# Modulation sums through turned 32x32 blocks on VectorE, and gate rows through DRAM, in a hybrid diffusion layer

## The chip, the cores and the metric

The kernel runs on one core of a Trainium2 chip. The metric is device time in microseconds (us) of one execution. A core has five engines that each follow their own instruction stream in order: TensorE (PE; its weight loads are listed apart, as PEld), VectorE (DVE), ScalarE (ACT), GpSimd (POOL) and SyncE (SP). DMA transfers are issued from queues on SP, ACT and POOL. An engine waits for another through semaphores.

## The reference

One layer for two groups of tokens, 256 context tokens (`x_prompt`) and 2048 latent tokens (`x_sample`), with model width 1024, all in float32. What matters here is the modulation. Each group has one conditioning vector, and a small matmul makes six vectors of 1024 numbers from it, which are used in every row of the group:

```python
def adaln(cvec, w_mod, b_mod):
    m = jax.nn.silu(cvec) @ w_mod + b_mod          # (1024,) @ (1024, 6144)
    return jnp.split(m[:, None, :], 6, axis=-1)

sh1, sc1, g1, sh2, sc2, g2 = adaln(c, w_mod[l], b_mod[l])
h = rms_norm(xs, norm1_g[l]) * (1 + sc1) + sh1
q, k, v, f = project(h, w_in[l], q_norm_g[l], k_norm_g[l])
...
mix = merge(attn, fourier_mix(f, w_four[l]), subln_g[l], lam_init, w_out[l])
xs = xs + g1 * mix
h = rms_norm(xs, norm2_g[l]) * (1 + sc2) + sh2
xs = xs + g2 * sq_relu_mlp(h, w1[l], w2[l])
```

The same is done for the context tokens with `c_ctx`. `sh1` and `sc1` are needed before the first projection, `g1` after the output projection, `sh2` and `sc2` for the second norm, and `g2` at the very end.

## The kernel before, in words

The 2304 tokens are 18 tiles of 128. The stages follow each other:

1. A short setup (to about 62 us) loads the first quarter of `w_mod`, makes modulation groups 0 to 3 (a group is 512 of the 6144 columns) and splits the projection weights.
2. The projection stage (about 62 to 468 us) runs a loop `for i in range(1, LAST)` over the tiles. A tile has four projections `proj(i, g)` of 24 matmuls each into four PSUM banks named `pj` (tag with four buffers), for q, k, v and the Fourier channels. Each float32 product is three matmuls of split operands (`mm3`, L87 to L89). The banks are read by `squares` (L250, L251, L254, the power on POOL at L255), `qk_norm` (`qn`, L268), `v_out` (L356) and `f_post`; when the next tile starts its projection 0, it needs the bank that `qn` of the tile before has read. Beside that the loop loads the next x tile, norms it (L187 to L191), transposes it (`pta`, L200), and stores q, k and v to DRAM.
3. The Fourier stage, attention (to about 1283 us), the output projection with the second norm (about 1283 to 1510 us), and a two-part MLP (the rest).

The loop of stage 2 is not in a written order: a scheduler lays out the instructions of each engine from a simulated timeline, so an edit can move neighbours. The output projection and the last part of the MLP stand under `tc.manual_schedule()`, where the order is that of the text.

Modulation groups 4 to 11 are made in stage 2, one in every odd tile i, by `mod_group_v`. VectorE multiplies each of eight row blocks of the weights (128x512) with a column of the conditioning vector and adds them up into `macc` (L164, L166), once for each of the two vectors s. What is left is the sum of `macc` over the 128 partitions. TensorE makes it: for each of four blocks of 128 columns a matmul with `macc` as weights and a column of ones as moving operand (L168) gives a column of 128 sums in `pm`. `mod_bias` (L142) adds the bias and puts the columns into `modc`, a 128x48x2 table: column c of it holds elements 128c to 128c+127 of the modulation vector.

The gates `g1` and `g2` multiply rows of tokens, so they are needed as a row of 1024 numbers repeated on all 128 partitions. `mk_gate` (L174 to L181) makes half a row: four matmuls, each with a column of `modc` broadcast to 128x128 as weights and the identity as moving operand, into a PSUM bank `pg`, and an ACT copy (L181) into the tile `g1[s]` or `g2[s]`. It is called four times in the output stage, between the matmuls `out_mm` (L1554, L1562, L1565, L1574) and four times early in the last stage (L1958). `out_post` (L1501) reads `g1`, `y_post` (L1902) reads `g2`.

Of the kernel before, what the change touches and what calls it, by code (L numbers as in the profile page):

```python
# [41 lines left out]
def body(tc, a, out):  # L42
    nc = tc.nc
    ctx = ExitStack()
    with ctx:
# [6 lines left out]
        def scratch(name, shape):  # L52
            return dram.tile(shape, F32, tag=name, name=name)
# [9 lines left out]
        four = scratch("four", [512, NT])  # L63
        xnew = [scratch(f"xnew{i}", [P, D]) for i in range(NT // P)]
        HB = NT // 2
        hop = [[scratch(f"hd{p}_{b}", [P, 4, 384]) for b in range(3)] for p in range(8)]
        tsum = [scratch(f"tsum{k}", [P, 3, 512]) for k in range(16)]
        sop = [[scratch(f"sd{p}_{b}", [P, 16, 384]) for b in range(3)] for p in range(8)]
# [71 lines left out]
        def mod_bias(gi, pm):  # L140
            b = cols[:, 32 + gi * 4:32 + gi * 4 + 4].unsqueeze(2).to_broadcast([P, 4, 2])
            nc.vector.tensor_add(modc[:, gi * 4:gi * 4 + 4, :], pm, b)  # L142
# [10 lines left out]
                nc.tensor.transpose(pm[:, j, :], r[0:2, j * P:(j + 1) * P], ident[0:2, 0:2])  # L153
            mod_bias(gi, pm)

        def mod_group_v(t2, pps, gi, w):

            pm = pps.tile([P, 4, 2], F32, tag="pm", name=f"pm{gi}")
            for s in range(2):
                acc = t2(f"macc{gi}_{s}")  # L160
                for k in range(KD):
                    wk, sc = w[k // 2][:, k % 2, :], cols[:, 8 * s + k:8 * s + k + 1]
                    if k == 0:
                        nc.vector.tensor_scalar_mul(acc, wk, sc)  # L164
                    else:
                        nc.vector.scalar_tensor_tensor(acc, wk, sc, acc, op0=ALU.mult, op1=ALU.add)  # L166
                for j in range(4):
                    nc.tensor.matmul(pm[:, j, s:s + 1], acc[:, j * P:(j + 1) * P], ones, start=True, stop=True)  # L168
            mod_bias(gi, pm)

        def mk_scale(dst, c0, gcol):
            nc.vector.tensor_scalar_add(dst, modc[:, c0:c0 + KD, :], 1.0)
            nc.vector.tensor_mul(dst, dst, cols[:, gcol:gcol + KD].unsqueeze(2).to_broadcast([P, KD, 2]))

        def mk_gate(pps, dst, c0, s, halves=(0, 1)):
            for hf in halves:
                pg = pps.tile([P, 512], F32, tag="pg", name=f"pg{c0}_{s}_{hf}", bufs=1)
                for j in range(4):
                    col = modc[:, c0 + hf * 4 + j, s:s + 1]
                    nc.tensor.matmul(pg[:, j * P:(j + 1) * P], col.to_broadcast([P, P]), ident, start=True, stop=True)  # L180
                nc.scalar.copy(dst[:, hf * 512:hf * 512 + 512], pg)  # L181

        def norm(pool, xt, nm, dst=None):

# [24 lines left out]
        with ExitStack() as c1:  # L209
# [28 lines left out]
            def proj(i, g):  # L238
                ps = pp.tile([P, 512], F32, tag="pj", name=f"pj{i}_{g}", bufs=4)
                hh, hl = HH[i]  # L240
                for k in range(KD):
                    mm3(ps, hh[:, k, :], hl[:, k, :], wh[g][k], wl[g][k], k == 0, k == KD - 1)
                PJ[i, g] = ps
# [172 lines left out]
            with tc.manual_schedule():  # L416
# [108 lines left out]
                v_split(1, 0, vo0, "v0")  # L525
                load(3)
            wm, LAST = None, N1 - 1
            for i in range(1, LAST):
                mg = 3 + (i + 1) // 2
                if i >= 2 + N1 // 2 - 1:  # L530
                    f_load(i)
                    if i > 2 + N1 // 2 - 1:
                        f_rev(i - 1)
                if i % 2 and mg < 12:
                    wm = mod_load(po, mg)
                if i > 1:
                    norm(p1, X[i + 1], f"a{i + 1}")
                    proj(i, 0)
                transposed(i + 1)
                if 1 < i < N1 - 2:  # L540
                    load(i + 2)
                squares(i, 0)
                if i > 1:
                    proj(i, 1)
                qk_T(i - 1)
                squares(i, 1)
                proj(i, 2)
                qk_post(i)
                v_post(i)
                proj(i, 3)  # L550
                f_post(i)
                if i % 2 and mg < 12:
                    mod_group_v(t2, pps, mg, wm)
                if i in (4, 6, 8, 10):
                    cache_tile((i - 4) // 2)
            mk_scale(scale2, 32, 88)
# [873 lines left out]
        with c3o, ExitStack() as c4, ExitStack() as c4x, ExitStack() as c4w:  # L1430
# [105 lines left out]
            with tc.manual_schedule():  # L1536
# [2 lines left out]
                mix_load(s1)  # L1539
                x_load(s0)  # L1540
                x_load(s1)
                w_split(1, 0, 1)
                mix(s0)
                w_split(1, 1, 4)
# [6 lines left out]
                    fn()  # L1551
                mix(s1)
                out_mm(s0, 1, 4)
                mk_gate(pp, g1[1], 16, 1, (1,))  # L1554
                w_split(0)
                kv_even.close()
                ms1 = ctx.enter_context(tc.tile_pool(name="m_s1", bufs=2, side="right"))
# [1 line left out]
                mix_load(s2)  # L1559
                x_load(s2)  # L1560
                out_mm(s1, 1)
                mk_gate(pp, g1[0], 16, 0, (1,))  # L1562
                out_post(s0, 1)
                out_mm(s0, 0)
                mk_gate(pp, g1[1], 16, 1, (0,))  # L1565
                out_post(s1, 1)
                mix(s2)
                out_post(s0, 0)
# [2 lines left out]
                mix_load(seq[3])  # L1571
                x_load(seq[3])
                out_mm(s1, 0)
                mk_gate(pp, g1[0], 16, 0, (0,))  # L1574
                out_post(s1, 0)
                x_store(s1)
                x_norm(s1)
# [284 lines left out]
        with ExitStack() as c6:  # L1862
# [62 lines left out]
            with tc.manual_schedule():  # L1925
                pend, NM, loaded, KS = None, 7 * 24, 4, []
                for i in range(7):
                    for b in range(3):
                        ps = [pp.tile([P, 512], F32, tag="ps", name=f"ps{i}_{b}_{j}", bufs=6) for j in range(3)]
                        for k in range(16):  # L1930
# [19 lines left out]
                            if (i, b) == (6, 2) and 9 <= k < 12:  # L1950
# [2 lines left out]
                                u = U3[6 + j]  # L1953
                                nc.vector.tensor_mul(u, u, g2[0][:, 0:512])
                                nc.vector.tensor_add(u, u, X[j])
                            if i == 0 and b == 1 and k in (2, 6, 10, 14):
                                s, hf = divmod(k // 4, 2)
                                mk_gate(pp, g2[s], 40, s, (hf,))  # L1958
                            KS.append((k, SO[m], TO[n]))
                            if i == 6 and b == 2 and 12 <= k < 15:  # L1960
                                continue
# [85 lines left out]
```

## Time and profile before

| | |
|---|---|
| median of 3 runs | 2914.43 us (2913.92 to 2915.5) |
| profiled execution | 2917.55 us, of which the span from first to last instruction is 2915.8 us |
| TensorE busy | 2877.5 us, 99% of the span |
| VectorE, ScalarE, GpSimd busy | 2022.7, 1564.2 and 1059.4 us |
| mean granted TensorE clock | 0.996 |
| chain that ended last | TensorE 91% |

How to read the rows that follow. A row of a timeline gives the start in us, the duration, engine, line of the kernel, operation, output<-input, shape and count; a bracket names how long the engine was idle before it and what ended that wait. A row of a group gives line, engine, operation, names, shapes, count, then busy us in total and mean ns of one, then idle time before it and its releasers. A row of a tile gives the least, median and largest duration in ns and the first and last start. Matmuls are pipelined, so the distance between two starts says more than a duration. A program matmul of float32 operands is two instructions in the trace.

### The profile page before, as it was taken

Reading aid. Unit: us, or ns where it says so; the run is one execution under the profiler, and the core shown is the slowest. Engines: PE = TensorE matmul, PEld = TensorE weight load, DVE = VectorE, ACT = ScalarE, POOL = GpSimd, SP = SyncE. Lnnn points to the kernel's source line nnn. Section 1 sums busy time; section 2 is a strip of 40 time slices with the busy share of each in tenths; the row PEclk is TensorE's granted clock in tenths of the full one; section 3 lists DMA queues with packets and bytes.
Section 4 is the critical chain, followed back from the end, with each engine's and each line's share of the span. In section 5 each row is a group of like instructions: output and inputs, shape, how many; then the busy total and the mean of one; then the engine's idle time right before and its main releaser. Section 6 shows DMA issues by size and latency. Waiting matters only on the chain.

```text
span 2915.8 us, 43832 instructions
## 1 busy us (share of the span) xinstructions
PE 2877.5 (99%) x15425; PEld 2501.2 (86%) x15425; DVE 2022.7 (69%) x3401; ACT 1564.2 (54%) x3524; POOL 1059.4 (36%) x865
## 2 busy tenths in 40 slices
PE   8999999999999999999999999999999999999999
PEld 4888888688888888888889999999998888888887
DVE  6666777989998988964468778778775344345554
ACT  4333323688998989964356566556554332232221
POOL 1111113398998999952213333333332000000000
PEclk9999999999999999999999999999999999999999
DMA  7777878621121201217777677676656364445663
GB/s 280 193 205 191 224 198 246 212 81 56 44 106 51 105 28 50 86 60 212 217 241 221 219 241 233 219 238 222 223 186 236 123 201 149 137 141 174 204 207 109
DMA packets 394415, 493.50 MB, mean 169 GB/s; under 512 B 26403, under 2 KB 307056, under 8 KB 391122
## 3 DMA queue, kind: packets, MB, share of 16 engines
q1 hardware_dynamic: 386560, 477.63, 52.0%
q10 hardware_dynamic: 4642, 7.88, 0.8%
q0 software_dynamic: 2992, 5.18, 0.6%
q8 instruction: 122, 2.00, 0.3%
q14 instruction: 99, 0.81, 0.1%
HBM read 313.11 MB, written 179.57 MB: 169 GB/s over the span
## 4 chain that ended last, share of the span: by engine, by line
PE 91%; DVE 3%; ACT 2%; DMA 1%; issue 1%; POOL 1%; SPq 0%; ACTq 0%; DVEq 0%; POOLq 0%
PE Ss L989 10%; PE ps L87 8%; PE ps L88 8%; PE ps L89 8%; PE pts L1044 4%; PE pj L87 4%; PE pj L88 4%; PE pj L89 4%; PE po L87 4%; PE po L89 4%; PE po L88 4%; PE pA L1654 2%; PE pA L1655 2%; PE pB L1655 2%; PE pB L1654 2%; PE pB L1656 2%
## 5 line engine op out<-in xcount | busy, mean ns | idle before, releaser
L994 DVE TENSOR_REDUCE mxs<-Ss 128x1 f32<-128x512 f32 x636 | 413.3, 685 | 65.2 <-PE Ss L989 53.0
L1329 DVE TENSOR_TENSOR sl<-sr,sh 128x768 fp32r<-128x768 f32 x168 | 161.8, 964 | 339.8 <-ACT sh L1328 339.3
L1029 POOL TENSOR_TENSOR P0s<-P0s,P1s 128x1024 f32<-128x1024 f32 (+2 forms) x128 | 377.0, 2945 | 10.7
L1328 ACT CAST sh<-sr 128x768 fp32r<-128x768 f32 x168 | 140.3, 836 | 424.7 <-PE ps L88 424.7
L1696 POOL TENSOR_TENSOR gs<-g,g 128x384 f32<-128x384 f32 x48 | 69.6, 1451 | 469.5 <-ACT g L1666 400.9
L1013 ACT ACTIVATE P1s<-Ss,mxs 128x512 f32<-128x512 f32 x318 | 215.4, 695 | 35.9 <-DVE mxs L997 34.5
L87 PE MATMUL pj<-wh,hh 128*128 128x512 f32 x576 | 229.6, 399 | 0.7 <-ACT fo L381 0.7
L88 PE MATMUL ps<-tlT,sh 128*128 128x512 f32 x585 | 229.3, 392 | 0.0
L87 PE MATMUL ps<-thT,sh 128*128 128x512 f32 x585 | 229.2, 392 | 0.0
L88 PE MATMUL pj<-wl,hh 128*128 128x512 f32 x576 | 227.7, 395 | 0.5 <-DVE wl L503 0.5
L89 PE MATMUL ps<-thT,sl 128*128 128x512 f32 x585 | 227.7, 389 | 0.0
L89 PE MATMUL pj<-wh,hl 128*128 128x512 f32 x576 | 226.6, 394 | 0.0
L1013 ACT ACTIVATE P0s<-Ss,mxs 128x512 f32<-128x512 f32 x318 | 214.4, 691 | 4.3 <-DVE mxs L997 3.6
L989 PE MATMUL Ss<-KS1s,Qs 128*128 128x512 f32 x636 | 196.4, 421 | 5.5 <-ACT P0s L1013 3.0
L989 PE MATMUL Ss<-KS0s,Qs 128*128 128x512 f32 x636 | 196.7, 422 | 2.6 <-ACT P1s L1013 2.4
L1044 PEld LDWEIGHTS pts<-ident,P0s 128*128 128x128 f32 x1280 | 158.2, 140 | 43.1 <-ACT ahs L1051 3.1
L1044 PE MATMUL pts<-ident,P0s 128*128 128x128 f32 x1280 | 191.0, 273 | 0.7 <-ACT P1s L1013 0.7
L1665 ACT ACTIVATE g<-uz 128x384 f32<-128x384 f32 x144 | 76.0, 528 | 200.1 <-DVE uz L1688 174.7
L1028 POOL TENSOR_SCALAR P1s<-P1s,tots 128x1024 f32<-128x1024 f32 (+2 forms) x128 | 172.0, 1344 | 5.8
L1056 DVE TENSOR_TENSOR als<-pts,ahs 128x512 fp32r<-128x512 f32 x256 | 165.9, 681 | 6.8 <-ACT ahs L1051 6.6
L87 PE MATMUL ps<-ophT,sh 128*128 128x512 f32 x423 | 165.9, 392 | 1.1 <-DVE uz L1688 1.1
L89 PE MATMUL ps<-ophT,sl 128*128 128x512 f32 x423 | 165.7, 392 | 0.0
(642 smaller groups left out, 8210.2 us busy)
## 6 DMA issues: line engine op xcount, KB each, us to landing
sr<-sd SPq DMA_DIRECT2D x84, 768.0 KB, 4.5
a<-in_w SPq DMA_DIRECT2D x184, 256.0 KB, 4.3
sd<-gs SPq DMA_DIRECT2D x192, 192.0 KB, 2.1
sd<-g SPq DMA_DIRECT2D x144, 192.0 KB, 4.5
wm<-in_w_mod SPq DMA_DIRECT2D x32, 512.0 KB, 5.7
Qs<-qd SPq DMA_DIRECT2D x32, 512.0 KB, 3.6
b<-in_w SPq DMA_DIRECT2D x64, 256.0 KB, 5.2
b<-tsum SPq DMA_DIRECT2D x64, 256.0 KB, 4.7
```

The lines of the kernel that those rows point to most:

```text
L87: nc.tensor.matmul(ps, lh, rh, start=first, stop=False)
L88: nc.tensor.matmul(ps, lh, rl, start=False, stop=False)
L89: nc.tensor.matmul(ps, ll, rh, start=False, stop=last)
L989: nc.tensor.matmul(S[:, :w], self.Q[:, x, m, j * P:j * P + P], self.hd.KS[m][:, b * 512:b * 512 + w], start=(x == 0), stop=(x == 1))
L994: nc.vector.tensor_reduce(self.mx[j][:, m, b:b + 1], self.S[j, m, b], axis=AX.X, op=ALU.max)
L1013: nc.scalar.activation(dst, S, AF.Exp, bias=self.mx[j][:, m, 6:7], accum_out=self.sm[j][:, m, b:b + 1])
L1028: nc.gpsimd.tensor_scalar(p, p, tot[:, 3:4], 0.0, op0=ALU.mult, op1=ALU.add)
L1029: nc.gpsimd.tensor_add(d, d, p)
L1044: nc.tensor.transpose(pt[:, c:c + P], self.p0[j][:, (kb + t) * P:(kb + t + 1) * P], ident)
L1056: nc.vector.tensor_sub(t, self.pt[kb], f32(self.A[kb][0]))
L1328: nc.scalar.copy(hi, src)
L1329: nc.vector.tensor_sub(lo, src, f32(hi))
```

## The change

`mod_group_v` keeps its accumulation on VectorE, and no longer uses TensorE. A `tensor_reduce` with `apply_transpose` takes `macc` as sixteen blocks of 32 columns; in each 32x32 block (32 partitions by 32 columns) it turns the block and sums, so that partition 32q+i of the output holds, for each block of columns c, the sum over the 32 partitions of quarter q of column 32c+i. The result is 128x16 for each s and goes into a tile `sums` that holds four groups.

What is left to add, over the four quarters, is done once for four groups, in tiles 8 and 16. `mod_sums` builds on GpSimd a 128x224 tile `quad`, zero but for four stacked 32x32 identities in columns 96 to 127 (a memset and three adds), and issues four matmuls, in which shifted windows of `quad` are the weights and every fourth column of `sums` (32 columns) is the moving operand. `mod_finish` adds the bias for all four groups in one VectorE instruction. `gate_store` transposes the sixteen gate columns of `modc` on TensorE, copies them on ScalarE, and stores them on ScalarE's queue, with one DMA for each s, to a scratch tensor `gates` in DRAM.

`mk_gate` and its eight calls go. Instead `gate_load` reads one row of 1024 numbers from DRAM with 128 partitions as destination, on SP's queue: two at the beginning of the output stage (behind the loads of the first x tiles, ahead of `mix_load(s2)`), and two in the last stage, at steps 2 and 10 of its second block.

```diff
+        gates = [scratch(f"gate{n}", [2, D]) for n in range(2)]
...
-        def mod_group_v(t2, pps, gi, w):
-            pm = pps.tile([P, 4, 2], F32, tag="pm", name=f"pm{gi}")
+        def mod_group_v(t2, sums, gi, w):
             for s in range(2):
                 acc = t2(f"macc{gi}_{s}")
...
-                for j in range(4):
-                    nc.tensor.matmul(pm[:, j, s:s + 1], acc[:, j * P:(j + 1) * P], ones, start=True, stop=True)
-            mod_bias(gi, pm)
+                nc.vector.tensor_reduce(sums[:, gi % 4, s, :], acc.rearrange("p (c i) -> p c i", i=32), axis=AX.X, op=ALU.add,
+                                        apply_transpose=True)
+
+        FIN = {}
+
+        def mod_sums(t2, pps, sums, gi):
+            z = t2(f"quad{gi}")[:, 0:224]
+            nc.gpsimd.memset(z, 0.0)
+            nc.gpsimd.tensor_add(z[:, 96:128], ident[:, 0:32], ident[:, 32:64])
+            for q in (2, 3):
+                nc.gpsimd.tensor_add(z[:, 96:128], z[:, 96:128], ident[:, 32 * q:32 * q + 32])
+            FIN[gi] = pm = pps.tile([P, 4, 2, 4], F32, tag="pm", name=f"pm{gi}")
+            for q in range(4):
+                nc.tensor.matmul(pm, z[:, 96 - 32 * q:224 - 32 * q], sums[:, :, :, q::4], start=(q == 0), stop=(q == 3))
+
+        def mod_finish(gi):
+            nc.vector.tensor_add(modc[:, gi * 4:gi * 4 + 16, :].rearrange("p (g j) s -> p g j s", j=4),
+                                 FIN.pop(gi).rearrange("p g s j -> p g j s"),
+                                 cols[:, 32 + gi * 4:48 + gi * 4].rearrange("p (g j) -> p g j", j=4).unsqueeze(3).to_broadcast([P, 4, 4, 2]))
+
+        def gate_store(t2, pps, n):
+            c0 = (16, 40)[n]
+            pr = pps.tile([P, 512], F32, tag="pg", name=f"pgate{n}")
+            gr = t2(f"gr{n}")
+            nc.tensor.transpose(pr[0:16, 0:P], modc[:, c0:c0 + 8, :].rearrange("p k s -> p (k s)"), ident)
+            nc.scalar.copy(gr[0:16, 0:P], pr[0:16, 0:P])
+            for s in range(2):
+                nc.scalar.dma_start(gates[n][s].rearrange("(k p) -> k p", p=P), gr[s:16:2, 0:P])
+
+        def gate_load(dst, n, s):
+            nc.sync.dma_start(dst, gates[n][s:s + 1, :].partition_broadcast(P).rearrange("p o d -> p (o d)"))
...
-        def mk_gate(pps, dst, c0, s, halves=(0, 1)):
...
@@ loop over the tiles of the projection stage
                 squares(i, 0)
                 if i > 1:
                     proj(i, 1)
+                fin = {8: 4, 16: 8}.get(i)
+                if fin:
+                    mod_sums(t2, pps, sums, fin)
                 qk_T(i - 1)
                 squares(i, 1)
                 proj(i, 2)
+                if fin:
+                    mod_finish(fin)
                 qk_post(i)
                 v_post(i)
                 proj(i, 3)
+                if fin:
+                    gate_store(t2, pps, fin // 8)
                 f_post(i)
                 if i % 2 and mg < 12:
-                    mod_group_v(t2, pps, mg, wm)
+                    mod_group_v(t2, sums, mg, wm)
@@ output stage
                 x_load(s0)
                 x_load(s1)
+                for s in (1, 0):
+                    gate_load(g1[s], 0, s)
...
                 out_mm(s0, 1, 4)
-                mk_gate(pp, g1[1], 16, 1, (1,))
...
                 out_mm(s1, 1)
-                mk_gate(pp, g1[0], 16, 0, (1,))
                 out_post(s0, 1)
                 out_mm(s0, 0)
-                mk_gate(pp, g1[1], 16, 1, (0,))
...
                 out_mm(s1, 0)
-                mk_gate(pp, g1[0], 16, 0, (0,))
@@ last stage
-                            if i == 0 and b == 1 and k in (2, 6, 10, 14):
-                                s, hf = divmod(k // 4, 2)
-                                mk_gate(pp, g2[s], 40, s, (hf,))
+                            if i == 0 and b == 1 and k in (2, 10):
+                                gate_load(g2[k // 8], 1, k // 8)
```

The scheduler lays stage 2 out anew. In its order for the changed program the two reduces of a group stand on VectorE ahead of L254 (the finish of the squares' sum) in tiles 2, 4, 6 and 16, and behind it in tiles 8 to 14; the four matmuls of `mod_sums` stand at the end of tile 8's last projection and inside tile 16's. The group loaded in tile i is finished in tile i+1.

7 lines of the change are left out of this document (1 added, 6 removed).

## The prediction

> **What bounds the kernel now.** I read the page first, then the busy time by stage, then the chain inside the stages that the change touches.
>
> ```profile
> PE 2877.5 (99%) x15425; PEld 2501.2 (86%) x15425; DVE 2022.7 (69%) x3401; ACT 1564.2 (54%) x3524; POOL 1059.4 (36%) x865
> PE 91%; DVE 3%; ACT 2%; DMA 1%; issue 1%; POOL 1%; SPq 0%; ACTq 0%; DVEq 0%; POOLq 0%
> 62.00:468.00 406.00, 405.31 (x1978) 337.39 (x1978) 281.19 (x523) 128.84 (x278) 64.87 (x32) 1.00 0.77 200
> 1280.00:1330.00 50.00, 49.17 (x256) 40.85 (x255) 30.20 (x46) 23.79 (x52) 10.98 (x12) 1.00 0.47 148
> 2270.00:2300.00 30.00, 30.00 (x141) 24.92 (x140) 10.89 (x14) 12.31 (x19) 0.00 (x0) 1.00 0.45 149
> ```
>
> In a window row the columns are the stretch, its length, the busy time of PE, weight load, DVE, ACT and POOL, then granted clock, DMA share and GB/s. TensorE carries 91% of the chain that ended last. In the projection stage (62 to 468 us) it is busy 405.3 of 406.0 us at full clock, while VectorE has 125 us free and ScalarE 277. The pieces of the change lie in this stage, at 1290 to 1311, and at 2261 to 2281. In all three a TensorE instruction taken out should bring the end nearer, unless something else is late next.
>
> ```profile
> by line: PE pj L87 29.8%; PE pj L89 29.7%; PE pj L88 29.6%; PE pta L200 3.5%; PE pm L168 3.3%; PE ptkT L310 1.7%; PE ptqT L310 1.7%; PE ptckT L310 0.4%; DVE fo L387 0.2%; ACT fo L381 0.1%; issue 0.0%
> 467.48 0.69 DVE L387 TENSOR_TENSOR fo<-fh,pj 128x512 f32<-128x512 f32 x1 [3.97 <-PE pj L89]
> ```
>
> The first line is the chain inside 62 to 468: TensorE throughout, the small modulation matmuls (L168) 3.3% of it. The second is the handover to the Fourier stage: VectorE had been idle 3.97 us waiting for the last projection. What the stage saves is therefore handed on.
>
> **Part 1: the modulation matmuls go.** Eight groups (4 to 11) each issue eight 128x1 matmuls, in the trace sixteen instructions.
>
> ```profile
> L168 PE MATMUL pm<-ones,macc x128: 165/250/250, 107.2 to 456.1; 128*128 128x1 f32 x128
> 106.94 0.39 PE L88 MATMUL pj<-wl,hh 128*128 128x512 f32 x1
> 107.17 1.84 PE L168 MATMUL pm<-ones,macc 128*128 128x1 f32 x16
> 108.87 0.48 PE L89 MATMUL pj<-wh,hl 128*128 128x512 f32 x1
> 109.19 0.39 PE L87 MATMUL pj<-wh,hh 128*128 128x512 f32 x1
> 94.79 0.87 PE pta L200 x8
> ```
>
> Starts are 0.23 apart in the stream (106.94 to 107.17). A group shifts the stream by 108.87 - 107.17 = 1.70, and the matmul after it takes 0.32 instead of 0.23, so 1.79 us. Eight groups: **-14.3 us**, all on the chain.
>
> In their place, after groups 7 and 11, come four matmuls with 32 columns (at two instructions each, eight) and one transpose. Their nearest rows: 1.70/16 = 0.106 us an instruction at one column, 0.87/8 = 0.109 at 128 columns (last line above, from the chain). Eight are 0.87, the transpose 0.11, two switches 0.09 each: 1.2 us, twice: **+2.4 us**.
>
> **Part 2: VectorE's reduces, and a wait that becomes tight.** VectorE gets sixteen reduces of 128x512 to 128x16 through turned 32x32 blocks, and loses six of eight small adds.
>
> ```profile
> L251 DVE TENSOR_REDUCE qss<-sq 128x8 f32<-128x512 f32 x34 | 23.0, 682 | 37.3 <-ACT sq L250 37.3
> L142 DVE TENSOR_TENSOR modc<-pm,cols 128x8 f32<-128x8 f32 x8 | 1.3, 158 | 1.0 <-PE pm L168 1.0
> L164 DVE TENSOR_SCALAR macc<-wm,cols 128x512 f32<-128x512 f32 x16 | 7.1, 482 | 0.0
> L166 DVE SCALAR_TENSOR_TENSOR macc<-wm,cols,macc 128x512 f32<-128x512 f32 x112 | 78.4, 747 | 15.8 <-DMA wm<-in_w_mod 15.8
> L255 POOL TENSOR_TENSOR qrs<-qss,mhalf 128x16 f32<-128x16 f32 x17 | 49.4, 2908 | 157.5 <-DVE qss L254 157.5
> ```
>
> The trace has no turned reduce. The plain one over the same 512 elements takes 0.68 us; I take that, with 0.48 as lower bound (L164's pass over 512) and 1.4 (two passes) as upper. 16 x 0.68 = 10.9 us against 125 us free: no throughput limit. But VectorE works in order, and after each tile's second projection its squares, their sum, the power on POOL (L255, 2.9 us) and `qn` (L268) must be through before TensorE may reuse the first of four `pj` banks for the next tile.
>
> ```profile
> 111.08 0.69 DVE L268 TENSOR_TENSOR qn<-pj,qrs 128x512 f32<-128x512 f32 x1 [1.87 <-POOL qrs L255]
> 114.69 0.39 PE L87 MATMUL pj<-wh,hh 128*128 128x512 f32 x1
> 211.35 0.69 DVE L268 TENSOR_TENSOR qn<-pj,qrs 128x512 f32<-128x512 f32 x1 [3.08 <-POOL qrs L255]
> 213.80 0.39 PE L87 MATMUL pj<-wh,hh 128*128 128x512 f32 x1
> 362.62 0.69 DVE L268 TENSOR_TENSOR qn<-pj,qrs 128x512 f32<-128x512 f32 x1 [3.09 <-POOL qrs L255]
> 363.92 0.47 PE L87 MATMUL pj<-wh,hh 128*128 128x512 f32 x1
> ```
>
> In each pair the bank comes free at the end of `qn` and TensorE starts on it in the next line. Slack: tile 2 114.69 - 111.77 = 2.9 us, tile 6 1.8, tile 12 0.6. The same pairs in tiles 4, 8, 10, 14 and 16 give 4.8, 2.1, 1.7, 3.8 and 4.7. Taking the L168 block out brings TensorE 1.79 us earlier to each of these points, and nothing in that chain gets faster. The order of the changed program puts the two reduces ahead of the sum's finish (L254) in tiles 2, 4, 6 and 16, which delays `qn` by 2 x 0.68 = 1.4; in tiles 8 to 14 they stand behind it and fit into the 3.1 us in which VectorE waits for POOL (the bracket above). New stalls: tile 2 1.79 + 1.37 - 2.9 = 0.2; tile 6 1.79 + 1.37 - 1.8 = 1.4; tile 10 0.1; tile 12 1.79 - 0.6 = 1.2; tile 8 none, since the new matmuls stand ahead of its bank. Sum **+2.9 us**. Bounds: 0 if the chain's start (an x load that TensorE's own transposes release) moves up too, 6 with the reduce at 1.4 us.
>
> **The rest of stage one.** POOL gets a memset and three 128x32 adds, twice.
>
> ```profile
> L815 POOL MEMSET jm<- 128x128 f32 x1 | 0.2, 233 | 0.0
> L694 POOL TENSOR_TENSOR ys<-yu 128x256 f32<-128x256 f32 x4 | 3.4, 843 | 0.0
> 317.84 0.33 ACTq L262 DMA_DIRECT2D rp<-in_rope  x1
> ```
>
> At most 0.4 + 3 x 0.84 = 2.9 us on an engine that is 16% busy and 341 us idle here; the next norm or `qrs` stands behind it, and the matmuls that need it come a whole projection later. Nothing, up to 1 us if `qrs` is caught behind it. ACT gets one copy and two DMA issues of about 0.4 (last line), twice; in the built program the second issue also waits for an earlier weight load. ACT's next work is the copies of `pj`, and it idled 277 us. Nothing. The new matmuls wait for the reduce of group 7 or 11 a projection (5.5 us) after it: nothing.
>
> **Part 3: the gate rows.** Eight halves of four matmuls (sixty-four instructions) and eight ACT copies go.
>
> ```profile
> 1290.36 1.05 PE L180 MATMUL pg<-ident,modc 128*128 128x128 f32 x8
> 1291.17 0.48 PE L87 MATMUL po<-woh,mh 128*128 128x512 f32 x1
> 1291.49 0.39 PE L88 MATMUL po<-wol,mh 128*128 128x512 f32 x1
> 1304.12 0.60 PE L1478 MATMUL po<-ident,am 128*128 128x128 f32 x4
> 1304.80 0.69 ACT L1479 ACTIVATE mT<-po,cols 128x512 f32<-128x512 f32 x1
> 1310.13 1.05 PE L180 MATMUL pg<-ident,modc 128*128 128x128 f32 x8
> 1311.82 1.09 PE L200 MATMUL ptb<-ident,xn 128*128 128x128 f32 x8 [0.63 <-DVE xn L191]
> L180 PE MATMUL pg<-ident,modc x64: 270/275/275, 1290.4 to 2280.7; 128*128 128x128 f32 x64
> 2271.00 0.89 PE pg L180 x8
> ```
>
> A half costs 1291.17 - 1290.36 = 0.81 plus 0.09 in the next matmul: 0.90 us. At the end the stream of four is unbroken: 4 x 0.90 = **-3.6 us**. In the output stage the first three stand ahead of the transposes at 1304.12, but the fourth stands in a stretch that ends with a wait: from 1304.72 (end of the transposes) runs mT, its split, out_post, norm, xn, and TensorE waited 0.63 us for it. Without the fourth half it only waits longer. 3 x 0.90 = **-2.7 us** (bounds -2.7 and -3.6).
>
> The rows come instead by four 512 KB loads on SP's queue.
>
> ```profile
> xo<-in_x_sample SPq DMA_DIRECT2D x1, 512.0 KB, 6.7
> 1281.64 0.43 SPq L1466 DMA_DIRECT2D am<-att  x1
> 1297.41 0.68 DVE L1501 TENSOR_TENSOR gt<-po,g 128x512 f32<-128x512 f32 x1
> L1902 DVE TENSOR_TENSOR c<-c,g x6: 691/692/694, 2353.9 to 2395.8; 128x512 f32<-128x512 f32 x6
> ```
>
> The first two take the place at 1281.64, ahead of am, mT and xo of the third tile, which move back by two issues of 0.43; am is first read at 1304. A load of that size lands in 6.7 us, the second near 1290; the first use is at 1297.41. Hidden, with 7 us over. The two at 2271 go between weight loads; the rows are first used at 2353.9. Nothing.
>
> **Sum.** -14.3 + 2.4 + 2.9 - 2.7 - 3.6 = -15.3 us. The profiled execution took 2917.55 us (its span 2915.8), 3.1 above the median of 2914.43; taken off the median: **2899.1 us**. By the bounds of the unknown terms: 2895.3 (no stalls, the fourth half counted) to 2902.2 (stalls of 6).
>
> **Rivals.** *Stage one keeps its length.* The chain of x load, squares, POOL and `qn` sets the pace of every pair of tiles, or the Fourier stage's own loads set when it starts, and all 11.9 us (14.3 - 2.4) are lost: 2914.4 - 6.3 = 2908.1. For it: the slacks of 0.6 to 2 us. Against: tiles 4, 14 and all without a group have 4 to 6 us, and VectorE waited 3.97 at the handover.
>
> *Slower: the turned reduce is dear.* A group's price X enters the chain twice; over the first seven pairs the stalls are about 7 x 1.79 + 14 X, less 3.09 hidden in four of them and 18.7 of slack: 14 X - 18.5 us. That eats the 18.2 us of the other terms at X = 2.6, and at X = 3.0 (4.4 times the plain row) the time is 2920. Per element nothing on VectorE in this trace is near that: 512 elements cost 0.48 to 0.75 us in every row. [...] No run here shows a turned reduce.
>
> *The gate loads are late.* They read one 4 KB row 128 times, which no load of this size in the trace does. TensorE stands still once they land after about 1303 (three `po` banks); at 30 us from issue instead of 6.7 it would lose 8 us: 2907.
>
> **Chances.** The sum 0.68 (its own range 2895 to 2902.5), stage one keeps its length 0.12, dear reduce 0.07, late loads 0.05, something unnamed 0.08. Within 0.2% (5.8 us), about what a measurement here can tell from no change, is 2908.6 to 2920.2: half of the second case and parts of the third and last, 0.09. Faster 0.82, slower 0.09. The range for 8 in 10 takes the sum's own bounds and the late loads: 2893.5 to 2907.
>
> **What would show it.** No L168 or L180 rows; TensorE's instructions down by about 170; turned reduces at 0.5 to 1.4 us; the projection stage 8 to 12 us shorter, with TensorE idle a few times before the first `pj` of a tile and `qn` as releaser (tiles 6 and 12 first); g loads landing before 1290 on the old clock; 3.6 us less in the last stage. The prediction is wrong if VectorE's reduces exceed 2 us, if the stall before `pj` appears in most tiles, or if the Fourier stage does not start as much earlier as the projections end.

## The result, and the profile after

The changed kernel takes 2908.06 us (median of 12 executions, 2905.58 to 2912.91). The kernel before took 2915.99 in the executions beside them (12, 2913.61 to 2918.93). The ratio is 0.9972, with a 95% interval of 0.9964 to 0.998: about 8 us less, where 15.3 were forecast, and 1.1 us above the range. The profiled execution took 2906.92 us, 1.1 below its median, with a span of 2905.1.

First the busy time on the page of the changed kernel, then two rows of its busy time by stage (the columns are those of the prediction), then the second stretch in the kernel before.

```profile
PE 2857.5 (98%) x15251; PEld 2482.1 (85%) x15251; DVE 2030.7 (70%) x3411; ACT 1557.9 (54%) x3518; POOL 1064.1 (37%) x873
```

```profile
62.00:468.00 406.00, 402.32 (x1907) 332.36 (x1906) 293.00 (x538) 130.69 (x282) 70.39 (x41) 1.00 0.77 202
468.00:560.00 92.00, 78.09 (x481) 66.20 (x479) 73.53 (x140) 40.35 (x95) 33.49 (x50) 0.93 0.81 262
```

```profile
468.00:560.00 92.00, 83.70 (x511) 72.39 (x509) 74.66 (x142) 39.67 (x90) 35.33 (x50) 0.94 0.82 260
```

TensorE has 174 instructions fewer and 20.0 us less to do, but the span is only 10.7 us shorter (and by the medians the time only 7.9, since the profiled execution before, 2917.55, lies 1.6 above its median). The second and third row show where to look: in the 92 us that hold most of the Fourier stage TensorE worked 5.6 us less than before, although nothing was taken out there.

The stage boundaries say it more exactly. These are rows of tiles (least, median and largest ns, then the first and the last start): the turned reduce; the first transposes after the projections (`ptqkT`), the first and last score matmul of attention (`Ss`), the first transposes of the second norm (`ptb`), the first matmul of the last stage (`tlT`), and the first of its last outputs (`cl`). First the kernel before, then the changed one.

```profile
L310 PE MATMUL ptqkT<-ident,qo x8: 270/272/273, 467.3 to 468.0; 128*128 128x128 f32 x8
L989 PE MATMUL Ss<-KS0s,Qs x636: 387/398/776, 555.7 to 1249.8; 128*128 128x512 f32 x159
L200 PEld LDWEIGHTS ptb<-ident,xn x136: 138/141/146, 1311.8 to 1504.7; 128*128 128x128 f32 x136
L88 PE MATMUL ps<-tlT,sh x585: 387/394/397, 2234.1 to 2909.4; 128*128 128x512 f32 x195
L1971 DVE TENSOR_TENSOR cl<-ps,g x3: 691/692/692, 2905.8 to 2911.4; 128x512 f32<-128x512 f32 x3
```

```profile
L167 DVE TRANSPOSE_TENSOR_REDUCE sums<-macc x16: 667/703/709, 107.0 to 446.2; 128x16 f32<-128x512 f32 x16
L331 PE MATMUL ptqkT<-ident,qo x8: 272/273/273, 459.0 to 459.8; 128*128 128x128 f32 x8
L1018 PE MATMUL Ss<-KS0s,Qs x636: 386/397/506, 553.2 to 1245.3; 128*128 128x512 f32 x159
L221 PEld LDWEIGHTS ptb<-ident,xn x136: 138/141/147, 1304.7 to 1497.7; 128*128 128x128 f32 x136
L89 PE MATMUL ps<-tlT,sh x585: 388/394/398, 2227.1 to 2898.7; 128*128 128x512 f32 x195
L1997 DVE TENSOR_TENSOR cl<-ps,g x3: 691/691/692, 2895.2 to 2900.8; 128x512 f32<-128x512 f32 x3
```

| up to | before | after | gained so far | in this stretch | forecast |
|---|---|---|---|---|---|
| first `ptqkT` | 467.3 | 459.0 | 8.3 | 8.3 | 9.0 |
| first `Ss` | 555.7 | 553.2 | 2.5 | -5.8 | 0 |
| last `Ss` | 1249.8 | 1245.3 | 4.5 | 2.0 | 0 |
| first `ptb` | 1311.8 | 1304.7 | 7.1 | 2.6 | 2.7 |
| first `tlT` | 2234.1 | 2227.1 | 7.0 | -0.1 | 0 |
| first `cl` | 2905.8 | 2895.2 | 10.6 | 3.6 | 3.6 |

Four of the six stretches come within 0.7 us of the forecast. The 2.0 us in attention were not forecast, and they do not follow the change: over the first 50 us of attention the granted clock was 0.97 in the kernel before and 1.00 in the changed one, and the longest `Ss` in the rows above took 776 and 506 ns. Of the kernels below, before_high and sums_high have a longest `Ss` of 776 ns, before_prep and gates_high of 506 and 505. From first to last `Ss` these last four take 694.1, 693.7, 692.3 and 692.0 us. The Fourier stage gives back 5.8 of the 8.3 us that the projections handed it. The place is found in the timeline of that stage; first the kernel before (GpSimd's first addition `ys`, L691, and two subtractions of VectorE that matter later), then the changed kernel (the issue of one store on SP's queue, the same addition, now L720, and the matmul that waited behind it).

```profile
507.93 0.74 POOL L691 TENSOR_TENSOR ys<-yd 128x256 f32<-128x256 f32 x1 [0.24 <-DVE yd L688]
508.48 0.73 DVE L579 TENSOR_TENSOR fpt0l<-etmp,fpt0h 128x512 fp32r<-128x512 f32 x1
508.63 1.19 POOL L692 TENSOR_TENSOR ys<-yd 128x256 f32<-128x256 f32 x1
509.14 1.23 DVE L579 TENSOR_TENSOR fpt1l<-etmp,fpt1h 128x512 fp32r<-128x512 f32 x1
```

```profile
493.74 0.37 SPq L370 DMA_DIRECT2D vd<-v17l  x1
498.83 0.53 POOL L612 DMA_DIRECT2D s<-in_s  x1 [0.32 <-DMA c<-in_c]
506.67 0.72 POOL L720 TENSOR_TENSOR ys<-yd 128x256 f32<-128x256 f32 x1 [7.31 <-DMA vd<-v17l]
510.11 0.79 PE L88 MATMUL pz<-abho,cwh 128*128 128x512 f32 x1 [4.17 <-ACT yu L706]
```

In the kernel before, GpSimd added as soon as `yd` was there. In the changed one it stood idle for 7.31 us until a transfer had landed that has nothing to do with the sum: the store of `v17l`, the low half of the last v tile, issued on SP's queue at 493.74. The copy `yu`, VectorE's next difference and TensorE's `pz` all waited behind it, TensorE for 4.17 us. The next rows of the changed kernel's busy time show what followed.

```profile
504.00:508.00 4.00, 1.94 (x14) 1.45 (x12) 0.00 (x0) 0.00 (x0) 1.33 (x2) 1.00 1.07 245
508.00:512.00 4.00, 1.65 (x3) 0.83 (x3) 1.81 (x3) 1.84 (x5) 4.00 (x7) 0.63 0.98 191
512.00:516.00 4.00, 3.12 (x5) 1.46 (x5) 4.00 (x6) 0.38 (x1) 4.00 (x5) 0.51 0.76 204
```

The column behind the busy times is the granted clock: 0.63 and 0.51 in the eight microseconds from 508 on, in the first two of which TensorE still stood.

Why a store and a sum that share no data meet is a matter of memory. In the built programs `ys0` occupies bytes 103392 to 111583 of every partition in both kernels; it is laid out when the projection stage's tiles are given up. From 109792 up lie the six buffers of the tag `t2r`, through which the halves of v, k and q are stored to DRAM. The first of the six, which `ys0` overlaps, held `qkT16_1h` last in the kernel before, and `v17l`, the last tile of this tag to be stored, in the changed one; in the kernel before `v17l` lay under `ys1`. Which buffer a tile gets follows from the order in which the scheduler's simulated timeline frees them, and with the change that order came out differently. The prediction looked at no addresses.

### The profile page after: what moved, and what is told of

Its sections match the earlier page's. It is cut to its first block, busy times and chain, and to the rows that moved or that the text cites. A ratio compares the mean times of both kernels' runs of the same rounds, so it can differ in the third digit from the quotient of the medians.

```text
span 2905.1 us, 43522 instructions
## 1 busy us (share of the span) xinstructions
PE 2857.5 (98%) x15251; PEld 2482.1 (85%) x15251; DVE 2030.7 (70%) x3411; ACT 1557.9 (54%) x3518; POOL 1064.1 (37%) x873
## 4 chain that ended last, share of the span: by engine, by line
PE 65%; issue 7%; POOL 4%; ACT 2%; DVE 2%; DMA 2%; SPq 0%; POOLq 0%; ACTq 0%; DVEq 0%
PE Ss L1018 10%; PE ps L89 8%; PE ps L88 8%; PE ps L90 8%; PE pts L1073 5%; PE po L90 4%; PE po L88 4%; PE po L89 4%; PE po L1099 2%; PE pB L1683 1%; PE pB L1682 1%; PE pB L1681 1%; PE pA L1682 1%; PE pA L1681 1%; POOL gs L1723 1%
## 5 line engine op out<-in xcount | busy, mean ns | idle before, releaser
L1058 POOL TENSOR_TENSOR P0s<-P0s,P1s 128x1024 f32<-128x1024 f32 (+2 forms) x128 | 378.7, 2959 | 10.7
```

The source lines that it names most:

```text
L1058: nc.gpsimd.tensor_add(d, d, p)
```

## The experiments

Theory A: this store holds the Fourier stage up. Theory B, a part of the prediction's first rival: the Fourier stage's own loads set when it starts, wherever its tiles lie. In all runs the kernel before ran beside them, with medians of 2915.7 to 2916.5 us.

**after_high: the overlap taken away.** The four `ys` tiles are laid out in the opposite order, so that `ys0` lies at the top and the two tiles written last meet `v17h` and `v17l`.

```diff
-            ys = [yp.tile([P, NS], F32, tag=f"ys{g}", name=f"ys{g}") for g in range(4)]
+            ys = {g: yp.tile([P, NS], F32, tag=f"ys{g}", name=f"ys{g}") for g in (3, 2, 1, 0)}
```

> The changed kernel with one line different: the four ys tiles of the Fourier stage are laid out in the opposite order, so that the first one written (ys0) no longer lies on the memory from which the last v17l tile of the projections is stored. Theory A (the store of v17l holds the Fourier stage up): the 7.31 us that POOL waited before its first L720 go, that addition starts at about 500 in place of 506.67, the attention's first Ss starts 5 to 7 us earlier than the changed kernel's 553.2 (546 to 548), and the time is 2908.1 - 5.8 = 2902.3 us (2900.5 to 2904). Theory B (the loads of the Fourier stage set when it starts, whatever lies where): first Ss at 553, time 2908 +- 1.5.

Measured: 2903.31 us (5 executions, 2901.12 to 2904.08), ratio to the kernel before 0.9955 (0.9941 to 0.9968). Two rows of tiles, then the timeline around the first additions, then one row of busy time, all of after_high:

```profile
L331 PE MATMUL ptqkT<-ident,qo x8: 271/272/273, 459.8 to 460.6; 128*128 128x128 f32 x8
L1018 PE MATMUL Ss<-KS0s,Qs x636: 387/397/505, 549.8 to 1241.8; 128*128 128x512 f32 x159
```

```profile
499.70 3.48 DVE L608 TENSOR_TENSOR fpt0l<-etmp,fpt0h 128x512 fp32r<-128x512 f32 x1
499.81 0.75 POOL L720 TENSOR_TENSOR ys<-yd 128x256 f32<-128x256 f32 x1
501.91 0.72 POOL L723 TENSOR_TENSOR ys<-yu 128x256 f32<-128x256 f32 x1
505.76 0.80 PE L88 MATMUL pz<-abho,cwh 128*128 128x512 f32 x1 [2.47 <-DVE yu L718]
```

```profile
504.00:508.00 4.00, 2.24 (x7) 1.95 (x8) 3.35 (x6) 0.00 (x0) 2.81 (x4) 0.72 0.74 177
```

One line of layout is worth 4.8 us, within what A expected (at its slower side), and outside B. In the built program the instructions of every engine stand in the order of the changed kernel, and only their waits differ; each of the five executions is faster than the fastest of the changed kernel's twelve. The first addition comes at 499.81 without a wait. But attention starts at 549.8, not at 546 to 548: the stage now takes 90.0 us (549.8 - 459.8), against 94.2 in the changed kernel and 88.4 before. The rows show a second wait behind the first. With GpSimd on time, its four additions (499.81 to 502.63) fall together with VectorE's `fpt0l`, which takes 3.48 us in place of the kernel before's 0.73; the difference, 2.75, is about the length of the four additions. TensorE waits 2.47 us for what VectorE does next, and again the clock falls, to 0.72 from 504 to 508.

**before_high and before_low: the layout without the change.** before_high is the kernel before with the same line. before_low exchanges `ys0` and `ys1` (order 1, 0, 2, 3), which puts `ys0` over `v17h` and `v17l`.

> The kernel before with the same one line (ys tiles in the opposite order). Its ys0 waited for no recent store, its ys1 overlaps v17h and v17l and started after an idle 2.17 us. Theory A: ys0 as before; ys1 up to 2.2 us earlier, so 2913.8 to 2916.0 (before: 2916.0). Theory B: 2916.0.

> The kernel before with ys0 and ys1 exchanged in memory, so that its first written tile overlaps v17h and v17l: the changed kernel's overlap without the change. Theory A: POOL's first L691 waits until the store of v17l has landed, which took at most 12.9 us from its issue in the changed kernel: 501.9 + 12.9 = 514.8 in place of 507.93, so the Fourier stage ends 3 to 7 us later (the 2.17 us ahead of ys1 go) and the time is 2919 to 2923. Theory B: 2916.0.

Measured: before_high 2916.23 us (11 executions), ratio 1.0001 (0.9992 to 1.001): the order by itself is worth nothing in the kernel before. before_low 2920.83 (11, 2916.09 to 2923.75), ratio 1.0017 (1.0008 to 1.0026): the overlap costs the kernel before 4.4 us. The rows of tiles of before_high and then of before_low, and the wait of GpSimd in before_low's profiled execution, which at 2916.09 was the fastest of its eleven:

```profile
L310 PE MATMUL ptqkT<-ident,qo x8: 270/272/273, 467.3 to 468.0; 128*128 128x128 f32 x8
L989 PE MATMUL Ss<-KS0s,Qs x636: 387/397/776, 554.5 to 1248.6; 128*128 128x512 f32 x159
```

```profile
L310 PE MATMUL ptqkT<-ident,qo x8: 270/272/273, 467.6 to 468.3; 128*128 128x128 f32 x8
L989 PE MATMUL Ss<-KS0s,Qs x636: 387/397/776, 554.1 to 1248.1; 128*128 128x512 f32 x159
```

```profile
POOL ys L691 <- DMA vd<-v17l: 2.1, 1, 2.1
```

The wait on the store is there, with 2.1 us, but in this execution it costs nothing: the stage takes 86.5 us (554.1 - 467.6), against 87.2 in before_high. That the slower ones waited longer fits the 4.7 us between this execution and the median, but no profile of one was taken, so the 4.4 us stand in the medians alone.

**prep_early, before_prep and after_prep: the second wait.** The two subtractions `fpt0l` and `fpt1l` read both operands from SBUF. In prep_early (on after_high) they are issued ahead of `yd` and `yu`, before GpSimd has anything to add; before_prep is the same edit on before_high, after_prep on the changed kernel with its own layout.

```diff
+                    if g == 1:
+                        prep(2)
                     if pend:
                         put(2048)(*pend)
                     pend = g, A[g], B
...
-                    if g % 2:
+                    if g == 3:
                         prep(2)
```

> after_high, and the two splits of the prompt's rows (fpt, L607/608) are issued ahead of the first yd and yu (L717, L718) in place of behind them. In after_high the first fpt0l took VectorE 3.48 us (0.73 in the kernel before) while GpSimd ran its four ys additions from 499.81 to 502.63; TensorE then waited 2.47 us for yu and ran on half the clock until about 508. Theory A1 (an addition of VectorE between two SBUF tiles waits while GpSimd's additions run, and that is why after_high got back only a part): fpt0l 0.7 to 1.3 us, no wait of 2.5 us, first Ss 2 to 4 us earlier than after_high's 549.8 counted from the stage's start, 2899 to 2901.5 us. Rival (the 3.48 us are a coincidence off the path, or the splits now wait for the load of fp): 2903 +- 1.5.

> before_high with the two fpt splits issued ahead of the first yd and yu: the edit of prep_early on the kernel without the change. If what prep_early gave back was time that the changed kernel had lost behind GpSimd (fpt0l and fpt1l took 0.73 and 1.23 us in the kernel before): 2916 (2914.8 to 2916.8). If the order of these splits is a gain of its own, with or without the change: 2913.

> The changed kernel with the early fpt splits alone, its ys tiles where the change left them. Theory A then A1 (the store of v17l holds GpSimd first, and only when that wait is gone do the splits collide with its additions): no gain, 2908 (2906.5 to 2909.5), GpSimd's wait for v17l still 5 to 7.5 us. If the two causes add up independently: 2905.

Measured: prep_early 2900.26 us (5, 2896.64 to 2901.15), ratio 0.9945 (0.9932 to 0.9957). before_prep 2913.82 (11, 2912.04 to 2915.58), ratio 0.9991 (0.9983 to 1.0). after_prep 2908.8 (11, 2906.23 to 2910.27), ratio 0.9974 (0.9965 to 0.9983). The rows of tiles and the timeline of prep_early, the rows of tiles of before_prep, and the wait in after_prep:

```profile
L331 PE MATMUL ptqkT<-ident,qo x8: 271/272/273, 457.2 to 458.0; 128*128 128x128 f32 x8
L1020 PE MATMUL Ss<-KS0s,Qs x636: 387/397/505, 542.7 to 1234.9; 128*128 128x512 f32 x159
```

```profile
494.73 0.68 DVE L608 TENSOR_TENSOR fpt0l<-etmp,fpt0h 128x512 fp32r<-128x512 f32 x1
495.33 0.68 DVE L608 TENSOR_TENSOR fpt1l<-etmp,fpt1h 128x512 fp32r<-128x512 f32 x1
497.28 0.75 POOL L720 TENSOR_TENSOR ys<-yd 128x256 f32<-128x256 f32 x1
497.85 0.68 DVE L717 TENSOR_TENSOR yd<-yu,pz 128x512 f32<-128x512 f32 x1
```

```profile
L310 PE MATMUL ptqkT<-ident,qo x8: 270/272/273, 467.5 to 468.3; 128*128 128x128 f32 x8
L991 PE MATMUL Ss<-KS0s,Qs x636: 386/397/506, 553.8 to 1246.1; 128*128 128x512 f32 x159
```

```profile
POOL ys L720 <- DMA vd<-v17l: 7.2, 1, 7.2
```

prep_early gains 3.0 us over after_high (its profiled execution, 2896.64, is the fastest of its five); the subtractions take 0.68 us each, and the stage 85.5 us (86.3 in before_prep). With both repairs the stage hands on what it gets: in these two executions the projections end 10.3 us earlier and attention starts 11.1 us earlier. The row at 497.85 is the counterpart: a difference that reads one operand from PSUM (`pz`) keeps its 0.68 us while GpSimd adds. In after_prep the same edit gains nothing: there GpSimd still waits 7.2 us for the store, so nothing collides. The two causes stand one behind the other, as expected.

The control was needed, and it missed its expectation. before_prep is 2.4 us faster than before_high, although in before_high's profiled execution the two subtractions took only 0.69 and 0.68 us, so that there was no such wait to take away. By the medians only the 0.6 us beyond this control belong to the change. But the profiles put the two gains in different places. Between before_high and before_prep, each profiled at its median, the Fourier stage differs by 0.9 us (87.2 and 86.3) and attention, which the edit leaves alone, by 1.8 (694.1 and 692.3, with the longest `Ss` named above). Between after_high and prep_early attention is alike (692.0 and 692.2), and the Fourier stage is 4.5 us shorter. The second wait is shown in the rows; how much of the 3.0 us it is worth is not.

**gates_high and sums_high: each half alone,** both on before_high. gates_high has the gate rows through DRAM and the old sums; sums_high has the turned reduces and the spread small matmuls, and `mk_gate`.

> before_high with the gate part alone: gate rows through DRAM in place of mk_gate, the modulation sums as they were (matmuls over the accumulators). By the prediction's terms 6.3 us less than before_high's 2916.2: 2909.9 (2908.5 to 2911.5). If the gate part's gain also hung on something else: 2913 to 2916.

> before_high with the modulation sums alone: turned reduces and the spread small matmuls, and mk_gate as before. By the prediction's terms 9.0 us less than before_high's 2916.2, if the Fourier stage hands it on: 2907.2. By what after_high showed (12.9 us less than before_high in all, 6.3 of them from the gates): 2909.6, since VectorE's wait behind GpSimd is there too. If the stage swallows it all: 2916.

Measured: gates_high 2909.14 us (11), ratio 0.9977 (0.9968 to 0.9986); sums_high 2907.93 (9), ratio 0.9974 (0.9965 to 0.9984). Against before_high that is 7.1 and 8.3 us less. Rows of tiles, gates_high first, then sums_high:

```profile
L315 PE MATMUL ptqkT<-ident,qo x8: 272/272/273, 467.1 to 467.8; 128*128 128x128 f32 x8
L996 PE MATMUL Ss<-KS0s,Qs x636: 387/397/505, 551.8 to 1243.8; 128*128 128x512 f32 x159
```

```profile
L326 PE MATMUL ptqkT<-ident,qo x8: 270/272/273, 456.5 to 457.2; 128*128 128x128 f32 x8
L1011 PE MATMUL Ss<-KS0s,Qs x636: 387/397/776, 547.4 to 1241.1; 128*128 128x512 f32 x159
```

The gate half gave about what was forecast (7.1 against 6.3), and its projections end where they did before (467.1). In its profiled execution, which at 2905.28 is the fastest of its eleven, 2.5 and 3.6 us of the gain lie in the two stretches from which the gate matmuls went (last `Ss` to first `ptb`, 59.5 us against 62.0 in before_high, and first `tlT` to first `cl`, 668.1 against 671.7). The Fourier stage (84.7 against 87.2) and attention (692.0 against 694.1), which this half leaves alone, were shorter as well. The sums' half gives between the two values expected: against before_high the projections end 10.8 us earlier (467.3 - 456.5), but attention starts only 7.1 earlier (554.5 - 547.4); the Fourier stage, at 90.9 us, kept 3.7 in this execution. The second wait stands there too:

```profile
L601 DVE TENSOR_TENSOR fpt0l<-etmp,fpt0h x1: 3126/3126/3126, 497.6 to 497.6; 128x512 fp32r<-128x512 f32 x1
```

The two halves add up to 15.4 us, and both together gave 12.9; with intervals of about 0.1% (3 us) on either side of each ratio that difference is not clear of the scatter.

**after_split: an attempt on the waits for `qn`.** On after_high, the second sample's sums and reduce of three groups move from tiles 1, 5 and 11 to the next, even tile.

```diff
+                if i - 1 in (1, 5, 11):
+                    mod_group_v(t2, sums, mg, wm, (1,))
                 if i % 2 and mg < 12:
-                    mod_group_v(t2, sums, mg, wm)
+                    mod_group_v(t2, sums, mg, wm, (0,) if i in (1, 5, 11) else (0, 1))
```

> after_high, and the second sample's eight weighted sums and its turned reduce of the groups loaded in tiles 1, 5 and 11 stand at the end of tiles 2, 6 and 12. These are the three places where the changed kernel's TensorE waited for qn, 3.0 us in all. If these waits were on the path to the end: 3.0 less than after_high, 2899.3 (2898 to 2901). If the time that they free is lost again before the attention, or the moved sums make new waits at tiles 3, 7 and 13: the time of after_high.

Measured: 2908.45 us (8), ratio 0.9973 (0.9963 to 0.9984), 5.1 above after_high, so both expectations missed. The expectation had the places wrong, too: the changed kernel's waits for `qn` stood in tiles 6, 10 and 12, and the longest, 2.05 us in tile 10, belongs to the group loaded in tile 9, which the edit does not move. First the waits of TensorE in the projection stage, then the end of that stage, then busy time around tile 8, all of after_split:

```profile
PE pj L88 <- DVE qn L289: 4.7, 3, 2.5
PE pm L181 <- DVE sums L167: 2.3, 1, 2.3
```

```profile
L331 PE MATMUL ptqkT<-ident,qo x8: 271/272/273, 467.8 to 468.5; 128*128 128x128 f32 x8
```

```profile
257.00:260.00 3.00, 0.67 (x6) 0.58 (x6) 2.30 (x5) 0.58 (x1) 1.82 (x1) 1.00 0.74 161
260.00:263.00 3.00, 1.64 (x8) 1.33 (x8) 1.85 (x4) 0.62 (x1) 1.09 (x1) 0.56 1.05 183
263.00:266.00 3.00, 3.00 (x9) 2.32 (x8) 3.00 (x9) 0.00 (x0) 0.00 (x0) 0.50 0.76 242
```

The moved sums make new waits: 2.3 us before the small matmuls of tile 8, which need group 7's reduce, and 4.7 for `qn`, 7.0 together against 3.5 in after_high. That is 3.5 us more, but the stage ends 8.0 later (467.8 against 459.8). The clock column holds the largest piece of the rest that the rows show: about half for six microseconds behind the two waits of tile 8. Of the 8.0 us the Fourier stage gives back 3.8: with the projections ending that late it takes 86.2 us (554.0 - 467.8) against 90.0, and `fpt0l` and `fpt1l` take 0.69 and 1.26.

**reduce_twice, reduce_thrice and prep_twice: the reduce's price.** The turned reduce is issued two or three times into the same place, on after_high and, doubled, on prep_early.

```diff
-                nc.vector.tensor_reduce(sums[:, gi % 4, s, :], acc.rearrange("p (c i) -> p c i", i=32), axis=AX.X, op=ALU.add,
-                                        apply_transpose=True)
+                for n in range(2):
+                    nc.vector.tensor_reduce(sums[:, gi % 4, s, :], acc.rearrange("p (c i) -> p c i", i=32), axis=AX.X, op=ALU.add,
+                                            apply_transpose=True)
```

> after_high with each turned reduce issued twice: 16 more of 0.70 us on VectorE, 1.41 us per group. If each wait for qn counts in full: the waits of TensorE for qn grow from 3.5 to 8 to 11 us (tiles 2, 6, 8, 10 and 12 by their slack), the stage ends 5 to 7 us later, 2908 to 2911 us; more if the clock falls after the longer waits. If VectorE's work in this stage is covered: 2903 +- 1.5.

> after_high with each turned reduce issued three times, 2.8 us more on VectorE per group than after_high. Waits of TensorE for qn: 3.5 us in after_high, 3.5 in reduce_twice; by the slack of the tiles 6 to 14 us here. If they count in full: 4 to 11 us over reduce_twice, 2902 to 2909. If VectorE's work in this stage is covered: 2898 to 2903.

> prep_early with each turned reduce issued twice. reduce_twice came out 5.3 us under after_high, although its projection stage ended later (461.1 against 459.8); its profiled execution, the slowest of its five, had fpt1l at 3.59 us. If its other executions were faster because the splits there got ahead of GpSimd, as prep_early makes them do always, then doubling the reduces costs here what it costs the projection stage: 2901 to 2904. If the doubled reduces make the program faster for another reason: 2895 (prep_early's 2900.3 less 5.3).

Measured: reduce_twice 2898.02 us (5, 2895.93 to 2904.27), ratio 0.994 (0.9926 to 0.9953); reduce_thrice 2905.91 (5), 0.996 (0.9946 to 0.9974); prep_twice 2899.98 (5, 2897.94 to 2901.66), 0.9946 (0.9934 to 0.9959). The grouped row of the reduces in prep_twice's projection stage, and the end of that stage:

```profile
L168 DVE TRANSPOSE_TENSOR_REDUCE sums<-macc 128x16 f32<-128x512 f32 x32 | 20.7, 690 | 0.0
```

```profile
L332 PE MATMUL ptqkT<-ident,qo x8: 272/273/273, 458.3 to 459.1; 128*128 128x128 f32 x8
```

Sixteen more reduces, 11 us of VectorE, moved the end of prep_early's projections by 1.1 us (458.3 against 457.2) and its time not at all (2899.98 against 2900.26). Both expectations for prep_twice missed, and so did both for reduce_twice: it came out 5.3 us under after_high, not above. Its profiled execution, the slowest of its five by 5.5 us, ended the projections at 461.1 and had `fpt1l` at 3.59 us. That its other executions escaped that collision is an argument, not shown. reduce_thrice ended its projections at 463.6, 3.8 later than after_high, with `fpt1l` at 3.74. Its time lies in the range expected if the waits count in full (2902 to 2909), but its waits for `qn` were 3.6 us, not 6 to 14, and its five executions fall into two groups, 2900.9 to 2902.0 and 2905.9 to 2906.3. So the price of a doubled reduce is far below what slack arithmetic gives, that of a tripled one is not clear, and why is open: every build with another number of reduces lays out the instructions of this stage anew. That such a build can gain 5.3 us for no reason found here is a warning for every difference of that size; the comparison of after_high with the changed kernel is free of it, because the order there is the same.

## Why the prediction was wrong, point by point

*The failed step* is the sentence at the handover, "What the stage saves is therefore handed on". The row of the handover (VectorE idle 3.97 us for the last projection) shows that the Fourier stage waits for the projections at its first instruction. It does not show that nothing else is late 40 us on. The prediction's own sign of being wrong watched the start of the Fourier stage; the time was lost behind that start, ahead of attention. In the executions profiled, 5.8 of 8.3 us went there. The runs showed the cause: the store of `v17l` under `ys0`. Taking the overlap away brings 4.8 us; giving it to the kernel before costs 4.4 in the medians. Of the 7.4 us between forecast and result (2908.06, against 2915.99 less 15.3, that is 2900.7) it accounts for about 5.

*What stays.* With the layout turned in both kernels the change is worth 12.9 us (2916.23 to 2903.31), with the early splits in both 13.6 (2913.82 to 2900.26). The 0.7 between these is within the scatter, and the last 1.7 us to 15.3 were not separated.

*The modulation matmuls and their successors.* Right: 174 instructions fewer where about 170 were said, no L168, and projections that end 8.3 us earlier in the changed kernel (7.5 to 10.8 in the other profiles with single, unsplit reduces) where 9.0 were forecast.

*The reduce.* Right in size: 0.703 us (median) against 0.68 taken from the plain reduce. The rival of a dear reduce, which needed 2.6 us, falls with that row.

*The waits for `qn`.* The sum was right, 3.0 us against 2.9, the places only in part: 0.73 in tile 6, 2.05 in tile 10 and 0.21 in tile 12, where 1.4, 0.1 and 1.2 stood, and none in tile 2. In tile 10 the reduces stood behind the sum's finish, as forecast; what was late was VectorE's work ahead of it, which had idled 2.98 us for a square on ScalarE in the norm of the next x tile (`nssa`, L209), where the kernel before shows no idle time. By these rows two thirds of the sum came from a wait that the prediction did not have, and that the total was right is luck. Nor is the arithmetic behind it borne out: by it a doubled reduce should have cost 5 to 7 us, and it cost none.

*Slips in the working.* The slacks listed for the first seven pairs add up to 17.7 us, not 18.7, which lowers by 0.07 us the price of 2.6 at which the dear reduce would have eaten the gain. And 512 elements did not cost 0.48 to 0.75 us in every row of VectorE: the `fpt1l` of the kernel before, shown above, took 1.23 us. Neither touches the sum.

*The gate halves.* Right: 2.6 and 3.6 us in the profiles, 2.7 and 3.6 forecast; alone, 7.1 us by the medians. The first `gt` starts at 1291.3 in the changed kernel, 6.1 us earlier than before, and no wait on a gate load stands there: the rival of late loads falls.

*The rival "Stage one keeps its length"* names 2908.1 us, which is the time measured. Its mechanism is not what happened: stage one became 8.3 us shorter, and after_high, whose loads are those of the changed kernel, starts attention earlier. Its second half, that something in the Fourier stage holds, was the right worry with the wrong object: a store of the stage before, not a load of its own. The chance of 0.12 was too small for a stage whose length had not been examined.

## What to carry to other kernels

Before a saving in one stage is counted at the end, look in the next stage for first writes into memory that the earlier stage frees, and ask which transfer last read that memory and when it lands; tiles that share no data meet there (`ys0` and `v17l`: 7.31 us of GpSimd), and an edit anywhere in the earlier stage can deal its buffers anew. Where a pool's order is free, put the tiles written first over the buffers that come free first (one line, 4.8 us here). And run the control of a repair on the kernel before as well: here it gained 2.4 us where 3.0 had been put down to the change.

## What the runs showed of the hardware

A subtraction of VectorE between two SBUF tiles took 0.68 us alone (prep_early), and 3.48 (after_high) and 3.59 (reduce_twice) with GpSimd's four additions beside it, each of which took 0.72 to 0.75. At the same place of the stage it took 3.13 in sums_high and 3.74 in reduce_thrice. In the kernel before, both sides stretched: two additions took 1.19 in place of 0.74, and the second subtraction 1.23. The difference `yd` at 497.85 in prep_early, with one operand in PSUM, kept its 0.68 while two additions of 0.75 and 0.74 ran. The long subtraction had started 0.11 us before the first addition in after_high and 0.22 before it in reduce_twice, and in both it stood through all four.

Behind some pauses of TensorE the granted clock was lower, and those cost more than their length. In the changed kernel it was 0.63 and then 0.51 in the eight microseconds around and behind the end of a pause of 4.17 us, and in after_high it was 0.72 in the four that hold most of a pause of 2.47. The length of the pause does not decide alone: reduce_twice paused 2.6 us ahead of the same `pz`, and the first `pabp` with `fpt0l` behind that took 0.28 us, where the one in after_high took 0.41. No run here shows what else decides.
